# The context side's pool opened in the routing's shadow, in place of an early ring of expert chunks

## The chip, the cores and the metric

The kernel runs on one core of a Trainium2 chip. The metric is the device time in microseconds of one execution, as a median of several runs. All data is fp32. TensorE (PE) multiplies, VectorE (DVE) and ScalarE (ACT) do the elementwise work, GpSimd (POOL) and SyncE (SP) here mostly issue transfers; SP issues those of the weights.

## The reference

Two blocks run one after the other on a sequence of 512 tokens of width 1024, each with a context of 256 tokens. The first block has a mixer (retention, window and neighbourhood attention) and then a feed-forward part with 16 experts, each of which chooses the 64 tokens that it rates highest:

```python
def expert_choice_ffn(h, w_router, w_gate, w_up, w_down):
    ...
    aff = jax.nn.softmax((h @ w_router).astype(jnp.float32), axis=-1)
    gate, idx = lax.top_k(jnp.swapaxes(aff, 1, 2), cap)
    ...
    xe = h[bidx, idx]
    hid = jax.nn.silu(jnp.einsum('becd,edf->becf', xe, w_gate)) * jnp.einsum('becd,edf->becf', xe, w_up)
    ye = jnp.einsum('becf,efd->becd', hid, w_down) * gate[..., None].astype(h.dtype)
    return jnp.zeros_like(h).at[bidx, idx].add(ye)
```

The second block has two layers. In each, the sequence and its own context are normalised and projected, and three branches (latent attention, pooling over 2 to 16 tokens, a gated linear scan) are merged. The first layer also gives a new context to the second. The context side of the first layer needs only the second block's own context input, nothing of the first block.

## The kernel before, in words

The program is written as Python generators that yield the cost of what they have just emitted. `weave(main, fill, ratio)` takes steps from a main generator and, after each, as much from a queue of fill work as the step's cost times the ratio. A scheduler then puts each engine's instructions in an order by its own priorities; each engine works through its queue in that order. Tiles come from pools with a fixed number of buffers for each tag, and a new tile waits until the last user of its buffer is done.

The stages around the change, in order:

- **The mixer of block 1** (`block1_mixer`), in pool `tpA`.
- **The routing** (`ffn_start`, `router`, `topk`). The 8 tiles x are scaled and shifted (L1268 DVE, L1269 ACT), multiplied with the router (L1209, PE), turned, and put through a softmax (L1219 to L1226). Then DVE finds the 64 best tokens of each expert in 8 rounds of MAX, MAX_INDEX and MATCH_REPLACE (L1240 to L1242) and makes indices of them (L1245 to L1257). The tokens are also turned and written to DRAM for the gathers (L1278 to L1282).
- **The experts** (`experts`), in 8 pairs. For each pair a gather fetches the chosen tokens (L1312, POOL), PE turns them (L1322), and 12 groups of matmuls follow (L1307): 4 for each half of gate and up, then 4 for the down projection. A group uses 4 chunks of weights of 512 KB (L1296, SP's queue), 48 chunks in a pair, 384 in all. Expert matmuls have a higher priority than the fill.
- **The context side of the second block's first layer** (`ctx2` with l = 0): input norm (L542, L545, L567 to L570), pooling branch (`poolb`, L1652 to L1672), attention, gated scan, output projection and norm (`finish`, L2002 and L2003). It is the fill of the experts' stage. Its weights come in chunks of 512 KB through a ring of 2 (L412, SP), are split into a high and a low part (L395 ACT, L391 DVE) in rings of 3, and multiplied in three products (L404 to L406), 24 matmuls of 256 columns for a chunk.
- **The join** (`ffn_end`): the experts' sums are turned and added to x (L1417 to L1421), and the first layer of block 2 is normalised (`xstart`).

Before, the expert chunks come from two rings: pool `tpR` holds an early ring of NEARLY = 20 buffers, which serves the first NPRE = 44 chunks, and `bigB` a ring of 8 for the rest. `tpR` stays open until the 44 chunks have been used; in that time experts run without fill. Only then pool `tpB` for the context side opens, and the rest of the experts is woven with it at RATIO_E = 0.8.

Of the kernel before, what the change touches and what calls it, by code (L numbers as in the profile page):

```python
# [7 lines left out]
F32 = mybir.dt.float32  # L8
# [226 lines left out]
def drain(g):  # L235

    while True:
        try:
            next(g)
        except StopIteration as e:  # L240
            return e.value
# [66 lines left out]
def weave(main, fill, ratio):  # L308

    while True:  # L310
        try:
            c = next(main)
        except StopIteration as e:
            return e.value
        fill.step(c * ratio)


class Kern:
# [9 lines left out]
    def pool(s, name, **k):  # L328
        return s.tc.tile_pool(name=name, bufs=1, reuse_waits="tile", **k)
# [956 lines left out]
    def experts(s):  # L1286
# [1 line left out]
        wx = s.d["wexp"]  # L1288

        def chunk(p, i, h):  # L1290
            if s.pre:
                s.pre -= 1
                w = s.early.tile([128, 1024], F32, name=s.uid("we"), tag="early", bufs=NEARLY)
            else:
                w = s.big.tile([128, 1024], F32, name=s.uid("we"), tag="wbig", bufs=s.nbig)
            nc.sync.dma_start(w, wx[p, i][:, h * 1024:h * 1024 + 1024])  # L1296
            return w

        def group(p, c0, stat, ps, kh):

            ws = [[chunk(p, c0 + e, h) for e in (1, 0)][::-1] for h in (1, 0)][::-1]
            with s.tc.high_priority(URGE):
                for h in range(2):
                    for kk in range(2):
                        k = 4 * kh + 2 * h + kk
                        for e in range(2):
                            nc.tensor.matmul(ps[64 * e:64 * e + 64, :], stat[:, k, 64 * e:64 * e + 64],  # L1307
                                             ws[h][e][:, kk * 512:kk * 512 + 512], start=k == 0, stop=k == 7)
# [801 lines left out]
def tags(w=512, **k):  # L2110
    return {a: b if isinstance(b, (tuple, str)) else (b, w) for a, b in k.items()}


PACE = (2, 2.5, 2.5)
NEARLY = 20
URGE = 600
NPRE = 44
LATE = True
XF = 1.0, 1.0
XM = 1.0  # L2120
# [8 lines left out]
GA = 1  # L2129
GX = 4  # L2130
RX = 2.5
TAGS_R = tags(t5=4)
TAGS_0 = tags(1024, u=6)
TAGS_A = tags(t=8, t5="t", y="u", pj=23, hx=16, hc=(16, 256))
TAGS_P = tags(P=(4, 640), PT=(2, 1152))
# [3 lines left out]
TAGS_M = tags(kc=(4, 256), P=(4, 768), PT=4)  # L2139
TAGS_F = tags(fx=8, ft=3)  # L2140
RATIO_G = 2
RATIO_E = 0.8
TAGS_G = tags(gh=8, gl=4)


def body(tc, d, out):
    from contextlib import ExitStack
    with ExitStack() as ctx:
        k = Kern(tc, ctx, d, out)
        pool = lambda n, **kw: ctx.enter_context(tc.tile_pool(name=n, bufs=1, **kw))  # L2150
        k.cp = pool("cp")
        k.wp = pool("wp")
        k.sp = pool("sp")
        k.pp = pool("pp", space=PSUM)
        k.dp = pool("dp", space=bass.MemoryType.DRAM)
        k.setup()
        M, C = [{}, {}], [{}, {}]
        xd, cd = k.dram([8, 128, 512]), k.dram([8, 128, 256])
        yp = pool("yp")
        k.base = (yp, TAGS_0)  # L2160
        with k.pool("tpA") as tp, ExitStack() as c2:
            k.where = (tp, TAGS_A)
            x, r = k.block1_mixer(xd, M, c2)
        k.kp = pool("kp")
        fill = Fill()
        k.nbig, k.pre = 8, NPRE
        big = ExitStack()
        k.big = big.enter_context(k.pool("bigB", side="right"))
        ex = k.experts()
        with k.pool("tpR") as k.early:  # L2170
            k.where = (k.early, TAGS_R)
            drain(k.ffn_start(x, r))
            while k.pre:
                next(ex)
        with k.pool("tpB") as tp:
            k.where = (tp, TAGS_C)
            k.wq = tc.nc.sync
            fill.add(k.ctx2(0, M[0], cd, C[0]))
            weave(ex, fill, RATIO_E)
            big.close()  # L2180
            k.where2 = (big.enter_context(k.pool("fe", side="right")), TAGS_F)
            x, acc = weave(k.ffn_end(xd), fill, RATIO_G)
            fill.flush()
            k.where2 = (None, {})
        k.where = (None, {})
        k.wq = tc.nc.sync
        k.gp = GX
        with k.pool("tpX") as tp:
            k.where = (tp, TAGS_X)
            p = k.xstart(0, M[0], C[0], x, acc, xd, fill, big.close)  # L2190
            f = k.xrest(0, M[0], C[0], *p, xd, None, fill)
            with k.pool("c1") as c1:
                k.where2 = (c1, TAGS_1)
                fill.add(k.ctx2(1, M[1], cd, C[1]))
                x, acc = weave(f, fill, 0.3)
                p = k.xstart(1, M[1], C[1], x, acc, xd, fill)
            k.where2 = (None, {})
            drain(k.xrest(1, M[1], C[1], *p, xd, out, fill))
# [18 lines left out]
```

## Time and profile before

| | us |
|---|---|
| three runs, median | 2788.2 |
| three runs, lowest and highest | 2779.96, 2794.11 |
| the profiled execution | 2794.44 |
| its span, first to last instruction | 2792.6 |

| engine | busy us | share of the span | instructions |
|---|---|---|---|
| PE | 2625.3 | 94% | 16372 |
| DVE | 1569.8 | 56% | 2957 |
| ACT | 1230.6 | 44% | 2159 |
| POOL | 161.0 | 6% | 260 |

PE's share is an average over stages that have different limits, so the stages are to be read one by one. The DMA share is the part of a stretch in which the core's 16 DMA engines were busy, as a mean; near 1 the transfers are the limit. A matmul of the program on fp32 operands of 512 columns shows as two in the trace where the operands are not split.

### The profile page before, as it was taken

How to read it: one execution, taken by the hardware profiler on the slowest of the kernel's cores; microseconds unless marked ns; L12 is line 12 of the kernel's file. 1: busy time of each engine (PE TensorE's matmuls, PEld its weight loads, DVE VectorE, ACT ScalarE, POOL GpSimd, SP SyncE). 2: the span in 40 equal slices, each digit the busy share in tenths (PEclk: the TensorE clock that was granted, in tenths of full speed). 3: DMA queues.
4: the chain of work that ended last, by engine and by line, in shares of the span. 5: the costliest groups of instructions: out<-in, count | busy, mean ns of one | idle time of the engine just before them, and what ended most of it. 6: DMA issues, size and time to landing. Idle time of an engine off the chain costs nothing. (4 is left out here: it accounts for less than half of the span.)

```text
span 2792.6 us, 41759 instructions
## 1 busy us (share of the span) xinstructions
PE 2625.3 (94%) x16372; PEld 1859.9 (67%) x16372; DVE 1569.8 (56%) x2957; ACT 1230.6 (44%) x2159; POOL 161.0 (6%) x260
## 2 busy tenths in 40 slices
PE   6999999999958999999998899999999999999997
PEld 2666677887633566555654577777777777777776
DVE  3564677676441324456232656656866546766974
ACT  3333355444222224365222444545655645555652
POOL 1000001110001000000000000000010000000001
PEclk9899999999979999999999899999999999999998
DMA  8545424634879999988999332213354332114353
GB/s 287 177 164 191 146 85 161 209 120 156 298 283 325 340 380 356 335 297 300 352 366 372 126 106 83 77 51 136 118 186 135 128 123 84 62 39 140 117 177 114
DMA packets 167974, 537.68 MB, mean 193 GB/s; under 512 B 21272, under 2 KB 22376, under 8 KB 167776
## 3 DMA queue, kind: packets, MB, share of 16 engines
q1 hardware_dynamic: 138528, 460.40, 47.2%
q0 software_dynamic: 17152, 52.57, 5.8%
q10 hardware_dynamic: 12096, 22.03, 2.1%
q8 instruction: 129, 2.11, 0.3%
q14 instruction: 69, 0.57, 0.1%
HBM read 484.06 MB, written 48.76 MB: 191 GB/s over the span
## 5 line engine op out<-in xcount | busy, mean ns | idle before, releaser
L391 DVE TENSOR_TENSOR wl<-wr,wh 128x1024 fp32r<-128x1024 f32 x320 | 390.8, 1223 | 386.8 <-ACT wh L395 357.3
L395 ACT CAST wh<-wr 128x1024 fp32r<-128x1024 f32 x320 | 334.4, 1047 | 458.2 <-PE ps L405 348.6
L404 PE MATMUL ps<-hx,wh 128*128 128x512 f32 x1168 | 473.8, 406 | 5.8 <-ACT hx L569 5.1
L405 PE MATMUL ps<-hx,wh 128*128 128x512 f32 x1168 | 468.8, 402 | 0.1
L406 PE MATMUL ps<-hx,wl 128*128 128x512 f32 x1168 | 466.9, 400 | 0.0
L404 PEld LDWEIGHTS ps<-hx,wh 128*128 128x128 f32 x1168 | 221.8, 190 | 66.9 <-issue 13.2
L1307 PE MATMUL ps<-we,xe 128*64 128x512 f32 x1024 | 241.1, 615 | 18.1 <-DMA we<-in_wexp 18.0
L405 PEld LDWEIGHTS ps<-hx,wh 128*128 128x128 f32 x1168 | 221.6, 190 | 52.3 <-issue 8.4
L406 PEld LDWEIGHTS ps<-hx,wl 128*128 128x128 f32 x1168 | 221.7, 190 | 50.2 <-issue 3.3
L673 ACT ACTIVATE P<-ps,st 128x768 f32<-128x768 f32 (+3 forms) x144 | 111.1, 771 | 142.6 <-DVE st L669 107.7
L1307 PEld LDWEIGHTS ps<-we,xe 128*64 128x64 f32 x1024 | 76.0, 141 | 144.8 <-issue 118.4
L404 PE MATMUL ps<-hc,wh 128*128 128x256 f32 x496 | 144.1, 291 | 0.1
L406 PE MATMUL ps<-hc,wl 128*128 128x256 f32 x496 | 139.8, 282 | 0.5 <-DVE wl L391 0.5
L405 PE MATMUL ps<-hc,wh 128*128 128x256 f32 x496 | 140.3, 283 | 0.0
L667 DVE TENSOR_REDUCE st<-ps 128x1 f32<-128x768 f32 (+3 forms) x144 | 114.2, 793 | 38.1 <-PE ps L406 35.3
L1307 PE MATMUL ps<-we,hT 128*64 128x512 f32 x512 | 122.8, 626 | 10.4 <-DMA we<-in_wexp 8.2
L695 PE MATMUL ps<-c_ident,P 128*128 128x128 f32 x688 | 110.0, 278 | 5.3 <-ACT PT L698 3.5
L404 PEld LDWEIGHTS ps<-hc,wh 128*128 128x128 f32 x496 | 94.1, 190 | 19.5 <-issue 14.2
L695 PEld LDWEIGHTS ps<-c_ident,P 128*128 128x128 f32 x688 | 79.9, 140 | 39.8 <-ACT PT L698 13.4
L471 PE MATMUL ps<-wm,sc_cc 128*32 128x512 f32 x384 | 89.4, 647 | 15.9 <-DMA wm<-in_wmod 14.1
L698 ACT COPY PT<-ps 128x512 f32<-128x512 f32 x123 | 70.1, 586 | 72.6 <-PE ps L695 71.9
L405 PEld LDWEIGHTS ps<-hc,wh 128*128 128x128 f32 x496 | 94.0, 190 | 4.0 <-issue 3.5
(517 smaller groups left out, 5036.1 us busy)
## 6 DMA issues: line engine op xcount, KB each, us to landing
we<-in_wexp SPq DMA_DIRECT2D x384, 512.0 KB
wr<-in_win SPq DMA_DIRECT2D x240, 512.0 KB
wm<-in_wmod SPq DMA_DIRECT2D x48, 512.0 KB
wr<-in_wbr SPq DMA_DIRECT2D x48, 512.0 KB
dram<-th ACTq DMA_DIRECT2D x72, 256.0 KB
mth<-dram SPq DMA_DIRECT2D x72, 256.0 KB
wr<-in_wout SPq DMA_DIRECT2D x32, 512.0 KB
dram<-mth POOLq DMA_DIRECT2D x48, 256.0 KB, 3.1
```

The source lines that it names most:

```text
L391: s.nc.vector.tensor_tensor(out, a, b, ALU.subtract)
L395: i = s.nc.scalar.copy(hi, src)
L404: t.matmul(out, a[0], b[0], start=start, stop=False)
L405: t.matmul(out, a[0], b[1], start=False, stop=False)
L406: t.matmul(out, a[1], b[0], start=False, stop=stop)
L471: nc.tensor.matmul(ps[32 * j:32 * j + 32, :], sc[:, k, :], w[:, j % 2 * 512:j % 2 * 512 + 512], start=k == 0, stop=k == 7)
L667: nc.vector.tensor_reduce(st[:, 0:1], sc[:, :n], AX.X, ALU.max)
L673: nc.scalar.activation(p[:, :n], sc[:, :n], AF.Exp, bias=st[:, 1:2], scale=scale, accum_out=st[:, 2:3])
L695: nc.tensor.transpose(tp[:, j:j + 128], blocks[(i + j) // 128], s.const("ident"))
L698: nc.scalar.copy(parts[i // 512][:, :m], tp[:, :m])
L1307: nc.tensor.matmul(ps[64 * e:64 * e + 64, :], stat[:, k, 64 * e:64 * e + 64], ws[h][e][:, kk * 512:kk * 512 + 512], start=k == 0, stop=k == 7)
```

## The change

The early ring and its pool go; all 384 expert chunks come through the ring of 8. The pool `tpB` opens right after the mixer, and the routing (`ffn_start`) is woven with the context side at a new RATIO_R = 0.8. The experts are then woven with it from their first group on, at RATIO_E = 0.55. In the changed program the lines from 1292 on stand 4 lower (L1307 is L1303, L1417 is L1413, L1658 is L1654).

```diff
-            if s.pre:
-                s.pre -= 1
-                w = s.early.tile([128, 1024], F32, name=s.uid("we"), tag="early", bufs=NEARLY)
-            else:
-                w = s.big.tile([128, 1024], F32, name=s.uid("we"), tag="wbig", bufs=s.nbig)
+            w = s.big.tile([128, 1024], F32, name=s.uid("we"), tag="wbig", bufs=s.nbig)
             nc.sync.dma_start(w, wx[p, i][:, h * 1024:h * 1024 + 1024])
...
-NEARLY = 20
...
-NPRE = 44
...
-TAGS_R = tags(t5=4)
...
-RATIO_E = 0.8
+RATIO_E = 0.55
+RATIO_R = 0.8
...
-        k.nbig, k.pre = 8, NPRE
+        k.nbig = 8
         big = ExitStack()
         k.big = big.enter_context(k.pool("bigB", side="right"))
         ex = k.experts()
-        with k.pool("tpR") as k.early:
-            k.where = (k.early, TAGS_R)
-            drain(k.ffn_start(x, r))
-            while k.pre:
-                next(ex)
         with k.pool("tpB") as tp:
             k.where = (tp, TAGS_C)
             k.wq = tc.nc.sync
             fill.add(k.ctx2(0, M[0], cd, C[0]))
+            weave(k.ffn_start(x, r), fill, RATIO_R)
             weave(ex, fill, RATIO_E)
```

DVE's queue at the end of the top-k, before: the last round (wk holds the affinities, vals the best eight) and the first of the index steps.

```order
L1240 MAX vals_6848<-wk_6781 16x8
L1241 MAX_INDEX idx<-vals_6848,wk_6781 16x8
L1242 MATCH_REPLACE wk_6781<-vals_6848,wk_6781 16x512
L1245 CAST idf_6874<-idx 16x64
L1254 TENSOR_SCALAR gate_6876<-ps_6880 64x8
L1255 CAST idx_6877<-ps_6880 64x8
L1256 COPY idxl_6879<-ps_6880 64x1
```

The same place in the changed program; pl, yp, pz and px are tiles of the context's pooling, wl the low part of a context weight.

```order
L1240 MAX vals_6946<-wk_6831 16x8
L1668 SCALAR_TENSOR_TENSOR pl_7090<-ps_7131,vh_6547,gs_7128 128x256
L1241 MAX_INDEX idx<-vals_6946,wk_6831 16x8
L391 TENSOR_TENSOR yp_7135<-pl_7090,yp_7134 128x256
L1242 MATCH_REPLACE wk_6831<-vals_6946,wk_6831 16x512
L1648 MEMSET pz_7177 128x8
L1649 MEMSET pz_7177 128x8
L1245 CAST idf_7191<-idx 16x64
L391 TENSOR_TENSOR wl_7212<-wr_7209,wh_7211 128x1024
L1654 TENSOR_TENSOR px_7181<-pz_7177 128x271
L1254 TENSOR_SCALAR gate_7193<-ps_7197 64x8
L1654 TENSOR_TENSOR px_7183<-px_7181 128x269
```

Between the rounds and the index steps now stand pooling steps and weight splits of the context side, here 7 of 12 rows.

SP's queue, before: the last context weights ahead of the experts' stream (wr is a context weight, we an expert chunk). From the third row on 84 expert chunks follow each other.

```order
L412 DMA wr_7517<-in_win 128x1024
L412 DMA wr_7600<-in_win 128x1024
L1296 DMA we_6912<-in_wexp 128x1024
L1296 DMA we_6914<-in_wexp 128x1024
L1296 DMA we_6916<-in_wexp 128x1024
```

The changed program, from the seventh of its first eight expert chunks to the ninth and tenth.

```order
L1292 DMA we_7290<-in_wexp 128x1024
L1292 DMA we_7292<-in_wexp 128x1024
L412 DMA wr_7209<-in_win 128x1024
L412 DMA wr_7304<-in_win 128x1024
L412 DMA wr_7368<-in_win 128x1024
L412 DMA wr_7445<-in_wbr 128x1024
L412 DMA wr_7464<-in_win 128x1024
L412 DMA wr_7545<-in_win 128x1024
L1292 DMA we_7352<-in_wexp 128x1024
L1292 DMA we_7354<-in_wexp 128x1024
```

Eight expert chunks stand ahead, where 84 stood, and then six context weights, before the stream goes on.

PE's queue at the last expert matmuls (ps<-we), before: behind them comes the join (fo is the sum of the experts, oh, ye and yl the last pair's part).

```order
L1307 MATMUL ps_12837<-we_12871,hT_12258 64x512
L1307 MATMUL ps_12837<-we_12869,hT_12258 64x512
L1417 MATMUL ps_12962<-c_ident,fo_12775 128x128
L1417 MATMUL ps_12962<-c_ident,fo_12777 128x128
L1417 MATMUL ps_12962<-c_ident,fo_12779 128x128
L1417 MATMUL ps_12962<-c_ident,fo_12781 128x128
L516 MATMUL ps_12938<-sq_12959,sqw 2x512
L1419 MATMUL ps_12963<-oh_12773,ye_12783 128x512
L1419 MATMUL ps_12963<-oh_12773,yl_12835 128x512
```

In the changed program: after the last two expert matmuls.

```order
L1303 MATMUL ps_12570<-we_12625,hT_12050 64x512
L1303 MATMUL ps_12570<-we_12623,hT_12050 64x512
L404 MATMUL ps_12668<-mh_12500,wh_12664 128x256
L405 MATMUL ps_12668<-mh_12501,wh_12664 128x256
L406 MATMUL ps_12668<-mh_12500,wl_12665 128x256
L404 MATMUL ps_12668<-mh_12504,wh_12664 128x256
L405 MATMUL ps_12668<-mh_12505,wh_12664 128x256
L406 MATMUL ps_12668<-mh_12504,wl_12665 128x256
```

And further down, where the join begins.

```order
L404 MATMUL ps_12848<-mh_12528,wh_12844 128x256
L405 MATMUL ps_12848<-mh_12529,wh_12844 128x256
L406 MATMUL ps_12848<-mh_12528,wl_12845 128x256
L1415 MATMUL ps_12896<-oh_12415,ye_12425 128x512
L1415 MATMUL ps_12896<-oh_12415,yl_12568 128x512
L1415 MATMUL ps_12916<-oh_12415,ye_12425 128x512
L1415 MATMUL ps_12916<-oh_12415,yl_12568 128x512
L497 MATMUL ps_12878<-ones,sq_12565 128x1 x2
L533 MATMUL ps_12884<-c_ident,rs_12881 128x128 x2
L1413 MATMUL ps_12895<-c_ident,fo_12417 128x128
```

Between these two pieces all rows are of the context's output projection (mh is the merged context, wh and wl a weight's parts): 144 matmuls of 256 columns, which before stood ahead of the last expert matmuls.

## Rows read from the trace of the kernel before

**Rows 1.** Page: the span.
```profile
span 2792.6 us, 41759 instructions
```

**Rows 2.** Stages: us, busy and count of PE, PEld, DVE, ACT, POOL; clock; DMA.
```profile
785.00:833.90 48.90, 19.72 (x96) 11.71 (x94) 25.96 (x69) 15.84 (x24) 2.02 (x2) 0.66 0.97 354
833.90:884.80 50.90, 46.16 (x211) 18.34 (x212) 4.47 (x8) 5.15 (x10) 5.31 (x9) 0.96 0.80 300
884.80:971.80 87.00, 73.43 (x401) 38.62 (x395) 30.24 (x72) 22.40 (x40) 9.69 (x10) 0.94 0.97 334
971.80:1062.10 90.30, 86.92 (x543) 54.50 (x541) 23.97 (x30) 23.46 (x34) 3.94 (x3) 1.00 1.00 378
1062.10:1151.60 89.50, 88.10 (x529) 52.43 (x527) 44.90 (x110) 42.21 (x93) 6.78 (x8) 1.00 0.94 338
1151.60:1252.10 100.50, 94.65 (x697) 55.62 (x697) 47.23 (x120) 51.28 (x109) 4.60 (x4) 0.97 0.90 319
1252.10:1352.80 100.70, 93.42 (x879) 56.10 (x877) 53.96 (x137) 50.47 (x112) 4.16 (x3) 0.97 0.89 310
1352.80:1443.50 90.70, 88.42 (x556) 55.66 (x554) 28.80 (x39) 22.25 (x31) 2.84 (x2) 1.00 0.99 362
1443.50:1536.40 92.90, 82.53 (x470) 46.85 (x470) 28.10 (x50) 24.44 (x44) 9.39 (x14) 0.96 1.01 371
1536.40:1564.60 28.20, 18.81 (x65) 7.33 (x65) 17.79 (x28) 11.03 (x18) 0.00 (x0) 0.83 0.34 121
```

**Rows 3.** Timeline of DVE and ACT in the routing: start, us, engine, line, [idle <-releaser].
```profile
789.61 4.91 DVE L1268 TENSOR_TENSOR x<-x,rb 128x512 f32<-128x512 f32 x8 [1.89 <-ACT rb L1264]
798.97 0.23 DVE L1219 COPY lo<-ps 128x64 f32<-128x64 f32 x1 [4.45 <-PE ps L1214]
...
802.50 0.68 DVE L1240 MAX8 vals<-wk 16x8 f32<-16x512 f32 x1 [1.78 <-ACT wk L1232]
...
822.27 0.17 DVE L1254 TENSOR_SCALAR gate<-ps 64x8 f32<-64x8 f32 x1 [0.70 <-PE ps L1253]
...
822.61 0.17 DVE L1257 CAST idx<-ps 64x16 uint32<-64x16 f32 x1
...
797.83 1.28 ACT L1223 ACT_TABLE_LOAD   x1
```

**Rows 4.** Timeline of PE: the first turn of tokens; one expert group.
```profile
831.99 1.94 PE L1322 MATMUL ps<-c_ident,xg 128*128 128x128 f32 x8 [9.76 <-DMA xg<-dram,idx]
...
1005.42 3.65 PE L1307 MATMUL ps<-we,xe 128*64 128x512 f32 x16 [1.17 <-DMA we<-in_wexp]
```

**Rows 5.** Timeline of PE: first and last of one projection's 24 matmuls.
```profile
1010.53 0.28 PE L404 MATMUL ps<-hc,wh 128*128 128x256 f32 x1
...
1013.24 0.28 PE L406 MATMUL ps<-hc,wl 128*128 128x256 f32 x1
```

**Rows 6.** Groups on DVE, 780 to 1565 us: count | busy, mean ns | idle before.
```profile
L391 DVE TENSOR_TENSOR wl<-wr,wh 128x1024 fp32r<-128x1024 f32 x73 | 89.0, 1224 | 112.9 <-ACT wh L395 100.6 <-PE ps L1307 5.7 <-PE ps L406 5.5
...
L567 DVE SCALAR_TENSOR_TENSOR nf<-c,A,rb 128x256 f32<-128x256 f32 x8 | 3.7, 481 | 1.0 <-ACT rb L557 1.0
L570 DVE SCALAR_TENSOR_TENSOR hc<-nf,mod,hc 128x256 fp32r<-128x256 f32 x8 | 3.7, 479 | 0.0
L2002 DVE SCALAR_TENSOR_TENSOR o<-o,G,rb 128x256 f32<-128x256 f32 x8 | 3.5, 480 | 5.4 <-ACT rb L557 5.4
...
L2003 DVE TENSOR_TENSOR o<-o,xr 128x256 f32<-128x256 f32 x8 | 3.0, 418 | 0.0
...
L1658 DVE TENSOR_TENSOR px<-pz 128x271 f32<-128x271 f32 x4 | 1.8, 440 | 5.2 <-ACT pz L1654 5.2
```

**Rows 7.** Waits of SP's queue in the eight pairs: us, times, longest.
```profile
SPq L1296 <- PE ps L1307: 348.7, 149, 16.6
```

**Rows 8.** Timeline of PE: the join's first turn, the next block's first matmul.
```profile
1540.02 0.66 PE L1417 MATMUL ps<-c_ident,fo 128*128 128x128 f32 x4 [3.64 <-DVE x L1421]
...
1564.58 1.65 PE L404 MATMUL ps<-hx,wh 128*128 128x512 f32 x3 [1.36 <-ACT hx L569]
```

## The prediction

> **What bounds the kernel now.** I read the span first [rows 1], then the table of stages [rows 2], which cuts the trace at the first and last expert matmul and at the end of each of the eight expert pairs. Its first row is the routing: 48.9 us in which PE is busy for 19.7 only, while the DMA engines are busy for 0.97 of the time, because they already fetch expert weights. The next eight rows are the pairs, 702.5 us together (833.9 to 1536.4). There two limits lie side by side. In the third, seventh and eighth pair the DMA engines have a share of 0.99 to 1.01 and move 362 to 378 GB/s: these are DMA bound. In the fourth, fifth and sixth their share falls to 0.89 to 0.94 while PE is busy for 88 of 89.5 us and 93 to 95 of 100: there the context side's work on PE is late. The first two rows (0.80 and 0.97) carry no context matmul at all, or few. The last row is the join after the experts, 28.2 us with PE busy for 18.8. Behind it PE is nearly full in both programs and nothing is moved, so the sum needs three terms: when the first expert matmul starts, how long the eight pairs take, and how long after them the join and what is left of the context take.
>
> A group of 4 chunks (2.1 MB) is 8 matmuls of the program, 16 of the trace, and takes PE 3.65 us [rows 4]; a pair has 12 groups, 43.8 us. A context projection of 24 matmuls of 256 columns runs from 1010.53 to 1013.24, with its last step 0.1165 us each [rows 5], and needs one chunk of 512 KB. DMA time of a chunk at 375 GB/s (the third and eighth pair's rates) is 1.40 us.
>
> **Start of the experts: +23 us.** Before, the chain from the normalised tiles to the first gather is DVE's, hardly with a pause: it starts at 789.61, waits 4.45 us for the logits, begins the top-k at 802.50 and has the index at 822.61 [rows 3]; then the gather keeps PE waiting for 9.76 us [rows 4]. The change puts the context's input norm, three pooling groups and their weight splits on the same DVE queue, in between these steps. DVE works in the order of its queue, so all that stands ahead of a routing step delays it; the later steps of the chain, the gather and the first expert matmul wait behind. Counted from the order, with the durations of [rows 6]:
> - up to the top-k: 8 scalings (0.48 each) and 4 of the 8 low halves (0.48), 5.8 us, and the table load for the exponential, 1.28 us, which ACT did in the wait for the logits [rows 3] and now does after the context's square root. The seven additions of squares fit into the 4.45 us. Sum 7.1.
> - inside the top-k: 4 low halves 1.9, 2 weight splits of 1.22, 11 steps on 256 columns of 0.42 to 0.48 (as L2003 and L567), 4.9, and 10 on a few columns, estimated at 0.1 each: sum 10.2.
> - between top-k and index: 2 weight splits 2.4 and 4 pooling steps and 2 edges, 2.1, less two waits that stood there, the longer 0.70 us: 3.3.
>
> These are 20.6; 2 to 3 us go to new waits on PE and ACT in this chain (pooling alternates between three engines), so **+23**: first expert matmul at 857. Bounds: all added DVE work is 23.7 us, and the chain's pauses (1.89, 4.45, 1.78 and 0.70 [rows 3], 8.8 together) could swallow some of it, so +15; with about a microsecond for each of a dozen handovers, +35. In exchange 144 of the context's matmuls (6 projections, 16.8 us of PE) are done in this shadow. The early ring is gone: 8 chunks of the experts are there at the start, where about 26 were (20 slots and 6 of the other ring).
>
> **The eight pairs: 702.5 to 683, -20 us.** The order of PE gives for each pair the context matmuls of 256 columns and the other small ones between its expert matmuls: before 0, 178, 326, 265, 248, 222, 345, 252; now 192, 216, 203, 193, 96, 180, 240, 228. Together 1548 for 1836: the lower ratio leaves 144 of them for after the experts, and 144 are in front. In chunks the DMA load hardly changes: 18 expert chunks more are still to come, 12 projections fewer, and the context's own inputs come earlier. What changes is that no pair is PE bound by the context's projections now. For each pair I take the larger of two times: PE = 43.8 + 0.1165 per context matmul + 0.125 per other one (from the fifth and sixth pair: 94.65 - 43.8 - 28.9 for 141, and 93.42 - 43.8 - 25.9 for 246); DMA = (chunks x 0.524 MB + 1.5 MB for gathers and scatters) / 375 GB/s. The same rule on the rows of before gives 90.9 for 90.3 (third), 88.4 for 90.7 (seventh), 94.65 for 100.5 and 93.4 for 100.7 (fifth and sixth, the gated scan, where small steps wait for each other): so I add 1.5 us, and 6.5 in the scan's two pairs. Now: chunks 56, 57, 56.5, 56, 52, 55.5, 58 and 49.5 (the last has 8 behind it and 2 MB of results more), DMA 82.3, 83.7, 83.0, 82.3, 76.7, 81.6, 85.0, 78.6; PE 69 to 74 but for the scan, where 222 and 148 other matmuls stand, 82.8 and 83.3. Sum with the additions 83.8 + 85.2 + 84.5 + 83.8 + 89.3 + 89.8 + 86.5 + 80.1 = **683**. The ring of 8 is no new limit: SP already waits for a freed slot 149 times [rows 7] and the third pair ran at 378 GB/s with it. Bounds: all bytes, 245 MB, at 378 GB/s are 648; no gain is 703.
>
> **After the experts: +22 us.** On PE the last 144 context matmuls (6 projections of the output) now stand in one row between the last expert matmul and the join: 16.8 us. Little of the join can run under them, since its matmuls are queued behind; only the 3.64 us in which PE waited for x [rows 8] go. Then the context's last norm comes (a wait of 5.4 us before, by the row of L2002 [rows 6]; ACT has less to do there now, I take 3), and its 16 DVE steps (3.5 + 3.0 us) are interleaved with the join's 16. DVE sets the join's length, so they count: 16.8 - 3.6 + 3 + 6.5 = 22.7, **+22**. Before, this stretch ran from 1536.4 to the first matmul of the next block at 1564.58 [rows 8]. Bounds: 13 (DVE's steps in gaps, and no norm wait) to 25.
>
> **Sum.** 23 - 20 + 22 = +25 us on the profiled execution's 2794.4 us (span 2792.6): 2819. That execution is 6 us above the median of the three runs, 2788.2; on the median the sum is 2813, and this I predict. About 0.5% (14 us) is what a measurement can tell from no change.
>
> **The rivals.**
> 1. *Streaming wins* (faster). The pairs come down to the byte bound, since PE has slack everywhere and small steps of the scan no longer meet full PE queues: 648. With a start at +15 and a join at +18 that gives -22: 2767. For it: the rates of three pairs. Against it: shares of 0.89 in the scan, where the price is waiting, not work. It decides if the pairs take less than about 657 us (then even the other two terms at their low bounds leave a gain). An extreme of it, 0.02 of its chance: DMA is no bound at all, and the pairs take PE's own times, 597 us, with 15 us of waiting: 2788 + 15 - 90 + 18 = 2731. Against that stands the third pair, whose 378 GB/s came with a DMA share of 1.00 [rows 2]. The Trainium skill, Perfetto Trace Analysis, section Roofline, says that a core alone on its memory is bounded by its 16 DMA engines at some 435 GB/s, 120% of its share of 358, which is the price list for this extreme: an estimate of 563 us for the pairs' bytes, less than PE needs. By that rule the engines at 378 still had room; the trace, which calls them fully busy there, doesn't agree.
> 2. *The terms cancel* (no change). DVE's pauses hide more, +15, the pairs take 675, the join +15: +2, 2790. For it: the pieces of PE work are the same in both, so only idle time can differ, and the idle routing is a third of what is idle in this stretch.
> 3. *The shadow is too short* (slower still). SP's queue now has six context weights between the first 8 expert chunks and the rest; they wait for split buffers, and with them the experts' stream. If the start comes at +35 and the pairs gain 10 only, +47: 2835.
> 4. *The change does nothing in the shadow*: the new pool's tiles wait for the tiles of the mixer that they replace. Then PE gets nothing before 833 and the lost prefetch, 18 chunks x 1.40 = 25 us, is the price: 2813, no other number than mine.
>
> **How the numbers follow.** Forecast with 4: 0.48; streaming wins 0.15; cancel 0.27; too short 0.10. Slower 0.58, same 0.27, faster 0.15. The range leaves out most of the first rival and the far end of the third: 2779 to 2838; the forecast's own is 2803 to 2826.
>
> **What would show it.** Right: the first expert matmul about 20 us or more after the routing's present end, DVE without a pause through it; DMA share in the routing well under 0.97; the scan's pairs near 89 us; 144 narrow matmuls in a row behind the last expert matmul, and some 50 us to the next block. Wrong: an index at most 10 us later; pairs of under 81 us; join steps of DVE that finish within 30 us.

## The result, and the profile after

The changed kernel takes 2816.8 us (median of 4 runs, 2815.7 to 2818.0), the kernel before 2791.2 in the runs beside it: a ratio of 1.0097, 95% interval 1.0073 to 1.0122. It is slower by about 26 us, where 25 were forecast. The profiled execution took 2815.7 us; from the page:

```profile
span 2813.8 us, 41706 instructions
```

The same table of stages as [rows 2] (stretch, its length, busy time and count of PE, PEld, DVE, ACT and POOL, granted clock, DMA share, GB/s), cut at the same events of the changed kernel: the routing, the eight pairs, and the stretch from the last expert matmul to the next block's first matmul.

```profile
783.00:845.80 62.80, 42.94 (x252) 34.02 (x250) 48.26 (x132) 31.52 (x57) 9.76 (x16) 0.79 0.60 198
845.80:920.30 74.50, 71.67 (x412) 39.17 (x411) 15.68 (x25) 12.99 (x20) 0.95 (x1) 0.99 0.97 351
920.30:1002.60 82.30, 74.74 (x429) 41.61 (x430) 18.93 (x24) 22.11 (x34) 3.87 (x3) 1.00 1.00 376
1002.60:1091.70 89.10, 81.69 (x455) 44.11 (x455) 36.40 (x96) 30.61 (x73) 6.76 (x8) 0.98 0.94 336
1091.70:1183.20 91.50, 82.76 (x442) 43.28 (x442) 27.53 (x56) 34.86 (x66) 4.64 (x4) 0.94 0.93 328
1183.20:1281.80 98.60, 81.02 (x716) 43.43 (x718) 49.51 (x139) 44.14 (x103) 3.88 (x3) 0.90 0.84 299
1281.80:1364.40 82.60, 78.24 (x641) 44.39 (x639) 30.37 (x73) 30.82 (x63) 3.89 (x3) 1.00 0.99 357
1364.40:1445.30 80.90, 74.75 (x440) 42.98 (x440) 20.29 (x28) 16.28 (x23) 2.84 (x2) 1.00 1.01 386
1445.30:1534.10 88.80, 77.49 (x429) 42.15 (x430) 23.95 (x35) 21.17 (x34) 7.73 (x11) 0.96 0.98 363
1534.10:1588.00 53.90, 41.21 (x226) 28.97 (x226) 31.33 (x56) 21.87 (x37) 1.61 (x3) 0.90 0.43 150
```

Read against [rows 2], the span's 21.2 us are four differences: the first expert matmul starts 11.9 us later (845.8 for 833.9), the eight pairs take 14.2 less (688.3 for 702.5), the stretch behind them 25.7 more (53.9 for 28.2), and all that follows 2.2 less. The medians lie 4 us further apart than these two executions.

**The routing.** DVE's busy time from its first routing step to the top-k, through the top-k, and from there to the index (columns: DVE, clock, DMA share, GB/s), before:

```profile
789.61:802.50 12.89, 6.20 (x14) 0.76 1.01 391
802.50:820.62 18.12, 17.33 (x40) 0.69 0.93 337
820.62:822.61 1.99, 0.80 (x8) 0.50 1.07 393
```

and in the changed kernel:

```profile
787.58:807.04 19.46, 13.78 (x35) 0.68 0.65 246
807.04:833.88 26.84, 24.45 (x67) 0.83 0.49 152
833.88:838.78 4.90, 4.79 (x19) 1.00 0.42 129
```

DVE's chain is 51.2 us long instead of 33.0, with 121 instructions in it instead of 62. Its idle time hardly changes (8.2 us for 8.7): what is added is work. The timeline of DVE shows how the context's steps lie in it (start, us, engine, line, operands, idle before and releaser):

```profile
805.06 0.47 DVE L567 SCALAR_TENSOR_TENSOR nf<-c,A,rb 128x256 f32<-128x256 f32 x1
805.46 0.47 DVE L570 SCALAR_TENSOR_TENSOR hc<-nf,mod,hc 128x256 fp32r<-128x256 f32 x1
805.85 0.47 DVE L567 SCALAR_TENSOR_TENSOR nf<-c,A,rb 128x256 f32<-128x256 f32 x1
...
807.04 0.68 DVE L1240 MAX8 vals<-wk 16x8 f32<-16x512 f32 x1
...
830.87 0.42 DVE L578 SCALAR_TENSOR_TENSOR gs<-gs,ps 128x256 f32<-128x256 f32 x1 [1.59 <-ACT gs L577]
...
833.88 0.17 DVE L1245 CAST idf<-idx 16x64 f32<-16x64 uint32 x1
...
838.78 0.17 DVE L1257 CAST idx<-ps 64x16 uint32<-64x16 f32 x1
```

The first three rows last 0.47 us each and start 0.40 us apart: a step's time in the trace overlaps the next one's start. The row of 830.87 is one of few waits: a context step waits for ACT, and the top-k's next round stands behind it.

PE behind the index, with the wait for the gathered tokens that was 9.76 us in [rows 4]:

```profile
843.92 1.94 PE L1318 MATMUL ps<-c_ident,xg 128*128 128x128 f32 x8 [4.68 <-DMA xg<-dram,idx]
845.79 2.57 PE L1303 MATMUL ps<-we,xe 128*64 128x512 f32 x8
```

**Behind the experts.** The stretch in three pieces (columns as in the table of stages), and PE's timeline in it:

```profile
1534.10:1544.00 9.90, 6.32 (x50) 5.91 (x50) 3.32 (x5) 4.27 (x7) 1.08 (x2) 0.97 0.85 319
1544.00:1558.10 14.10, 13.96 (x95) 13.96 (x96) 6.37 (x9) 6.54 (x11) 0.54 (x1) 0.78 0.53 174
1558.10:1588.00 29.90, 20.93 (x83) 9.10 (x82) 21.65 (x44) 11.06 (x20) 0.00 (x0) 0.94 0.24 82
```

```profile
1542.88 0.39 PE L404 MATMUL ps<-mh,wh 128*128 128x256 f32 x1 [2.97 <-ACT wh L395]
...
1544.14 0.58 PE L406 MATMUL ps<-mh,wl 128*128 128x256 f32 x1 [0.76 <-DVE wl L391]
1544.52 0.42 PE L404 MATMUL ps<-mh,wh 128*128 128x256 f32 x1
1544.74 0.42 PE L405 MATMUL ps<-mh,wh 128*128 128x256 f32 x1
...
1557.46 0.28 PE L405 MATMUL ps<-mh,wh 128*128 128x256 f32 x1
1557.58 0.28 PE L406 MATMUL ps<-mh,wl 128*128 128x256 f32 x1
...
1588.01 1.65 PE L404 MATMUL ps<-hx,wh 128*128 128x512 f32 x3 [1.36 <-ACT hx L569]
```

The 144 narrow matmuls fill 1534.1 to 1558.1: 24.0 us, and the join behind them takes 29.9, where it took 28.2 alone. Twice PE waits for a weight (2.97 and 0.76 us). After the waits the matmuls start 0.21 us apart, at 1557 they start 0.117 apart: the granted clock of the second piece is 0.78, a mixture of the two levels (1.2 and 2.4 GHz).

### The profile page after: what moved, and what is told of

Its sections match the earlier page's. It is cut to its first block, busy times and chain, and to the rows that moved or that the text cites. A ratio compares the mean times of both kernels' runs of the same rounds, so it can differ in the third digit from the quotient of the medians.

```text
span 2813.8 us, 41706 instructions
## 1 busy us (share of the span) xinstructions
PE 2636.4 (94%) x16372; PEld 1865.2 (66%) x16372; DVE 1566.8 (56%) x2957; ACT 1228.9 (44%) x2155; POOL 159.5 (6%) x260
## 5 line engine op out<-in xcount | busy, mean ns | idle before, releaser
L1303 PE MATMUL ps<-we,xe 128*64 128x512 f32 x1024 | 243.2, 616 | 31.9 <-DMA we<-in_wexp 30.7
L1303 PEld LDWEIGHTS ps<-we,xe 128*64 128x64 f32 x1024 | 72.5, 141 | 161.3 <-issue 123.4
L1303 PE MATMUL ps<-we,hT 128*64 128x512 f32 x512 | 122.4, 623 | 6.1 <-DMA we<-in_wexp 4.3
L404 PEld LDWEIGHTS ps<-hc,wh 128*128 128x128 f32 x496 | 96.3, 195 | 32.9 <-issue 25.6
L406 PEld LDWEIGHTS ps<-hc,wl 128*128 128x128 f32 x496 | 96.3, 194 | 5.4 <-DVE wl L391 4.2
```

The source lines that it names most:

```text
L404: t.matmul(out, a[0], b[0], start=start, stop=False)
L406: t.matmul(out, a[1], b[0], start=False, stop=stop)
```

## The experiments

The theory: three terms add up. The routing becomes longer on DVE's queue and the prefetch is lost; the pairs have a floor in their bytes, so that less fill in them saves only part of its work; and what is left over behind the experts is paid in full. Ratios are against the kernel before, in runs beside each; differences to the changed kernel are between medians. Rows are of one execution of each kernel, whose routing can begin some us earlier or later than another's.

### The leftover put back among the experts

```diff
-RATIO_E = 0.55
+RATIO_E = 0.6
```

> The changed kernel with one number other: the fill's share in the experts is 0.60 instead of 0.55, so that none of the 144 narrow context matmuls is left over behind the experts; they lie within the eight pairs, most of them in the second half. Theory (the three terms add; the leftover is paid in full, a pair pays for fill only where its PE work is above its bytes or its waits): from the end of the experts to the next block's first matmul 54 us falls to 28 to 32; the eight pairs grow from 688 by 0 to 10 us; the start stays within 2 us of 846; 2817 - 24 + 6 = about 2799. Rival (PE's work is conserved, so the 144 cost the same wherever they stand): pairs grow by 17 to 24, about 2814.

Measured: 2801.0 us, ratio 1.0040 (1.0025 to 1.0056), 15.8 below the changed kernel. The pairs, and the stretch behind them:

```profile
844.30:1545.80 701.50, 640.96 (x4111) 359.09 (x4110) 234.20 (x501) 223.35 (x436) 36.49 (x38) 0.97 0.95 346
1545.80:1574.00 28.20, 17.41 (x67) 7.16 (x65) 18.69 (x31) 10.19 (x17) 0.00 (x0) 0.85 0.48 167
```

The 53.9 us are 28.2 again, exactly the length before. The pairs grow by 13.2, more than the theory's 0 to 10 and less than the rival's 17 to 24. So one narrow matmul costs 0.092 us among the experts (13.2 / 144) and 0.178 behind them (25.7 / 144). The time agrees with the theory, though the pairs hide less than it said. The higher ratio also moves other fill from later pairs to earlier ones, so the two prices are averages.

### The spread taken away

```diff
-RATIO_E = 0.55
+RATIO_E = 0.8
```

> The changed kernel with 0.80 instead of 0.55 as the fill's share in the experts, as in the kernel before: the fill is used up after six of the eight pairs, and nothing is left over behind them. It takes the spread away and keeps the pool's early opening. Theory (a pair costs the larger of its bytes and its PE work, and pairs without fill cannot go under their bytes, 78 to 80 us): the first six pairs grow by 60 to 80 us together against share 0.60, the last two shrink by 15 to 20; pairs 725 to 740 instead of 701, 28 us behind them, 2820 to 2838. Rival (only the sum of the work counts, not its spread): 2801, as with 0.60.

Measured: 2842.1 us, ratio 1.0192 (1.0169 to 1.0215). The fourth pair, the last two, and all eight:

```profile
1118.50:1233.20 114.70, 100.03 (x969) 60.36 (x969) 62.19 (x172) 61.08 (x142) 4.16 (x3) 0.90 0.78 266
1422.30:1504.50 82.20, 54.47 (x212) 17.25 (x211) 9.53 (x21) 5.76 (x9) 4.75 (x5) 0.90 0.95 331
1504.50:1585.50 81.00, 55.23 (x212) 18.09 (x212) 4.76 (x7) 5.83 (x8) 5.08 (x6) 0.89 0.91 329
844.70:1585.50 740.80, 652.76 (x4111) 364.47 (x4110) 236.63 (x505) 226.05 (x440) 37.03 (x38) 0.95 0.93 329
```

The same 4111 matmul records as with 0.60, and 39.3 us more in the pairs. Against 0.60 the first six pairs take 52 more (577.6 for 525.5, where 60 to 80 were expected) and the last two 13 less (163.2 for 176.0, where 15 to 20 were). The rival falls: the place of the fill counts. A pair without fill has PE busy for 55 us and still takes 81 to 82, 10 more than my prediction's rule for 48 chunks (26.7 MB at 375 GB/s, 71). The ring of 8 streams at 330 GB/s there, and PE waits for chunks for 48.2 us in the two pairs. The time is 4 us above the expected range.

### Nothing in the shadow

```diff
-RATIO_E = 0.55
-RATIO_R = 0.8
+RATIO_E = 0.634
+RATIO_R = 0.0
```

> The changed kernel without any fill in the routing's shadow (share 0 there), and 0.634 in the experts so that about the same is left over behind them (168 narrow matmuls). Theory (the shadow's fill makes the routing longer on VectorE's queue and earns little later): the first expert matmul is 10 to 14 us earlier (832 to 836), the pairs 5 to 12 us longer than 688, the leftover's 24 more matmuls 3 us: about 2816, the same as the changed kernel. Rival (the shadow's fill is worth its PE time, 144 matmuls of 0.117 us and the splits with it): about 2833. Second rival (the shadow only costs): 2805.

Measured: 2820.2 us, ratio 1.0108 (1.0090 to 1.0125), 3.4 above the changed kernel, with intervals that overlap. Routing, pairs, and the stretch behind:

```profile
785.00:831.30 46.30, 18.38 (x80) 10.87 (x80) 27.96 (x72) 16.39 (x29) 4.21 (x7) 0.62 0.55 201
831.30:1531.60 700.30, 637.40 (x4082) 353.49 (x4081) 243.74 (x529) 225.57 (x440) 37.33 (x38) 0.98 0.95 344
1531.60:1591.80 60.20, 45.69 (x253) 32.72 (x251) 32.66 (x57) 23.92 (x40) 2.15 (x4) 0.83 0.44 149
```

The start comes 14.5 us earlier, the pairs are 12.0 longer, and the 24 further leftover matmuls cost 6.3 (I had put 3). That is the theory: the shadow gives about as much in the pairs as it takes in the routing. The 3.4 us are no more than the larger leftover costs, so the fill in the shadow is worth nothing that can be measured.

### The routing's steps first

```diff
-            nc.vector.max(vals[0:16, q], wk[0:16])
+            with s.tc.high_priority(URGE):
+                nc.vector.max(vals[0:16, q], wk[0:16])
...
```

All top-k and index steps on DVE (L1240 to L1257), and the four small matmuls between them (L1252, L1253), get the expert matmuls' priority, so that they stand ahead of the fill.

> The changed kernel with the routing's top-k and index steps put ahead of the fill's splits in VectorE's order; the same fill in each stretch. Theory (the splits between the top-k steps lengthen the routing, and the routing is the path): the top-k part falls from 26.8 us towards the 18.1 of the kernel before, the index from 838.8 to 829 to 833, the first expert matmul from 845.8 to 837 to 840; the pairs keep 688 within 3: about 2810. Rival (the experts are bound by bytes that could not arrive earlier, so an earlier start only adds waiting in the first pairs): the pairs grow by the 6 to 8 us gained, 2817.

Measured: 2816.4 us, ratio 1.0090 (1.0075 to 1.0106): no gain that is shown. The index comes 5.6 us earlier, near what the theory wanted, 1.0 of it because the routing itself begins 1.0 earlier:

```profile
833.17 0.17 DVE L1261 CAST idx<-ps 64x16 uint32<-64x16 f32 x1
```

But the first expert matmul starts at 844.35, only 1.4 earlier. PE's queue:

```profile
842.30 0.67 PE L1672 MATMUL ps<-pl,pw 128*128 128x256 f32 x2
842.81 0.60 PE L1323 MATMUL ps<-c_ident,xg 128*128 128x128 f32 x4
844.35 1.94 PE L1308 MATMUL ps<-we,xe 128*64 128x512 f32 x8 [0.94 <-DVE xe L1324]
```

PE now goes from the context's matmuls straight into turning the gathered tokens, with no wait for them. They had landed at 838.8, 4.0 us before: the fill in PE's queue is what came last. Both theory and rival miss the place: the earlier index was eaten between the index and the first expert matmul, not in the first pairs. These rows are of the fastest of the six executions (2809.9 us); its pairs are 4.5 us shorter than the changed kernel's (683.8 for 688.3), a gain that the medians do not show.

### The prefetch alone

```diff
-NEARLY = 20
+NEARLY = 8
```

in the kernel before.

> The kernel before with one thing of the change alone: the early ring has 8 buffers instead of as many as fitted, so 12 of the chunks that were in memory before the first expert matmul are not; the fill is spread as before. Theory (the experts' stretch is bound by bytes, so each chunk fetched ahead is worth its transfer): the first expert matmul stays within 3 us of 834; the pairs grow from 702 by 12 x 1.40 = 17 us; about 2808. Rival (the pairs are bound by PE and by waits on it, the prefetch is immaterial): 2791 within 4.

Measured: 2808.9 us, ratio 1.0061 (1.0043 to 1.0079), the time that the theory had. The first pair, all pairs, and PE's wait for the gather:

```profile
829.00:898.80 69.80, 51.51 (x211) 16.92 (x212) 4.47 (x8) 5.36 (x10) 5.87 (x10) 0.91 0.83 295
829.00:1549.60 720.60, 659.17 (x4267) 377.67 (x4266) 261.73 (x566) 242.01 (x472) 45.23 (x53) 0.97 0.95 339
```

```profile
827.14 1.94 PE L1322 MATMUL ps<-c_ident,xg 128*128 128x128 f32 x8 [5.77 <-DMA xg<-dram,idx]
```

The pairs grow by 18.1, all of it in the first (69.8 for 50.9). PE waits for chunks there for 16.6 us instead of 4.1, and the expert matmuls take 49.1 instead of 43.9, at a granted clock of 0.91 instead of 0.96. By the first expert matmul 16 chunks had been issued, where before 26 had: 10 fewer, and not 12, so 1.40 us for each would be 14. At the same time the wait for the gather falls from 9.76 [rows 4] to 5.77, and the first expert matmul comes 4.9 us earlier (829.0), which the theory, with 834 within 3, did not have.

### Both: the prefetch kept, the pool opened earlier

```diff
-NPRE = 44
+NPRE = 20
...
-RATIO_E = 0.8
+RATIO_E = 0.72
```

in the kernel before; the second kernel has 28 and 0.74.

> The kernel before, with its early ring of 20 buffers, but each buffer used once (20 chunks instead of 44 pass it), so that the context's pool opens inside the first pair rather than behind it, and 0.72 instead of 0.80 as the fill's share, so that the fill spreads over more of the experts and none is left over. Theory (prefetch is worth 1.40 us a chunk, spreading is worth something only where a pair is bound by PE, the routing stays free of fill): the first expert matmul at 829 to 834, the eight pairs 688 to 703, 28 us to the next block: 2775 to 2790. Rival (the fill's spread is worth nothing): 2790 within 4. Second rival (more chunks ahead delay the gather's rows further): start 838, 2795.

> As b_p20 with 28 chunks through the early ring and 0.74 as the fill's share: the context's pool opens about two thirds into the first pair. Theory: between the kernel before and b_p20, 2778 to 2790. Rival (opening inside the first pair costs a wait of the ring): above 2795.

Measured: 2798.0, ratio 1.0033 (1.0019 to 1.0047), and 2785.7, ratio 0.9987 (0.9971 to 1.0003). The first is a miss. Its experts start at 830.6, as the theory had it and not at the second rival's 838, but its first pair takes 65.1 us instead of 50.9, and the wait for the gather is longer too:

```profile
828.76 1.94 PE L1322 MATMUL ps<-c_ident,xg 128*128 128x128 f32 x8 [12.02 <-DMA xg<-dram,idx]
```

PE's waits for chunks in the first pair, in the kernel with 20, in that with 28, and in the kernel before (line, releaser: us, times, longest):

```profile
PE ps L1307 <- DMA we<-in_wexp: 10.5, 3, 4.1
PE ps L1307 <- DMA we<-in_wexp: 3.9, 1, 3.9
PE ps L1307 <- DMA we<-in_wexp: 4.1, 1, 4.1
```

By the first expert matmul 28, 26 and 26 chunks had been issued, so the longer waits do not come from less being fetched ahead. With 20 the early buffers are not used again, and SP issues nothing between 821.9 and 851.0; before, and with 28, the next chunk goes out at 836.4 and 835.3. So the early ring is worth its buffers by their second use in the first pair, and not only by what it fetched ahead. These waits are 6.4 of the 14.2 us. The rest is fill in that pair (24 context matmuls and those of the input norm, 4.0 us) and expert matmuls at a lower granted clock (47.5 us for 43.9, at 0.90 for 0.96).

With 28 the first pair holds no context projection, just as before, and takes 56.9. That is not for want of chunks: PE waits 2.1 us for the context's input norm, whose matmuls take 1.2, and the expert matmuls take 46.0 us at a clock of 0.91.

In the kernel with 20 the seven other pairs gain 7.7 us (643.9 for 651.6), and the stretch behind loses 4.3 (32.5 for 28.2). With 28 the time is the lowest of all here, but its interval holds 1: no gain that is shown. Its profiled execution, 2794.1 us, is one of its slower ones.

### The join's steps first

```diff
         for k in range(9):
+            up = s.tc.high_priority(URGE)
+            up.__enter__()
             if k < 8:
...
                 s.sqrow(ps, x[k - 1], w[:, k - 1, :], k - 1, "ft")
+            up.__exit__(None, None, None)
```

The turning, the additions to x (L1413, L1415, L1417), the squares and, in the same way, the norm's steps behind them get the expert matmuls' priority.

> The changed kernel with the steps of the experts' end (combine, residual, norm) put ahead of the leftover's splits in VectorE's order; the 144 narrow matmuls stay behind the experts. Theory (in the 54 us the matmuls take 24, and the splits between the end's steps 6 to 8): the 54 us become 45 to 49, 2809 to 2813. Rival (the matmuls and their weights' splits are the path and the end's steps have slack): 54 stays, 2817. The floor, if the matmuls hid wholly under the end's steps: 28, 2791.

Measured: 2811.1 us, ratio 1.0080 (1.0058 to 1.0101), in the range of the theory, though the interval overlaps with the changed kernel's; and the stretch shrinks by 3.0 only (50.9, where 45 to 49 were expected). In two pieces, up to the last narrow matmul and from there:

```profile
1535.80:1559.00 23.20, 19.82 (x149) 19.22 (x148) 10.39 (x13) 10.85 (x17) 1.61 (x3) 0.93 0.71 245
1559.00:1586.70 27.70, 19.78 (x82) 9.65 (x80) 21.02 (x44) 11.18 (x20) 0.00 (x0) 0.88 0.25 85
```

The matmuls take 23.2 (24.0 in the changed kernel) and the join 27.7 (29.9), one after the other as before. So the interleaved DVE steps cost 2 us, not the 6 to 8 of the expectation, and the matmuls' own row is the rest. The other 3 us of the 5.7 lie outside this stretch and are not explained.

## Why the prediction was right, point by point

**The whole.** Slower by 26 us with 25 forecast, and the three terms have their signs and their order: start +11.9 (forecast +23), pairs -14.2 (-20), behind the experts +25.7 (+22). The sum is closer than its parts: the start was too high by 11, the two others too low by 6 and 4. That these errors cancel to 2 us is luck. Along the experiments' medians the change is a smaller ring, +19 (2789.8 to 2808.9); the pool opened early, with the fill in the shadow and over all pairs, -8 (to 2801.0); and 144 matmuls left over, +16 (to 2816.8). The first two steps are not pure: with the small ring 16 chunks are issued ahead, in the changed kernel 8.

**Start, the term most mis-sized.** The chain on DVE came out as counted in kind: 18.2 us longer where 20.6 were summed: 6.6 up to the top-k (7.1), 8.7 in it (10.2), 2.9 behind (3.3). Each piece is a little short of the sum, since durations of the trace overlap the next start (0.47 long, 0.40 apart); for the 59 added instructions that is a few us. The 2 to 3 us for new waits were no extra: they took the place of old pauses (8.2 us idle for 8.7). What the sum lacked is the gather. I carried its 9.76 us over unchanged, although I wrote that the early ring's transfers would be gone: from the index to the first expert matmul there are now 7.0 us instead of 11.3, and the first gather lands 4.8 us after its issue instead of 8.4. The kernel with the small ring and no other change shows the same, 7.3, and the one with more fetched ahead shows 13.5. The Trainium skill, DMA: Bandwidth & Descriptors, section Queues, rings and completion order, says that each DMA engine takes turns between its queues packet by packet, by which a gather shares the engines with the stream; PE's waits of 4.68 and 5.77 us with a thinner stream and of 9.76 and 12.02 with a full one agree in direction, and no run shows single packets. The last 2 us of the start lie ahead of the change's steps: the routing itself begins 2.0 us earlier, and in the eight other kernels' traces it begins between 784.2 and 790.4, so this difference may be chance.

**The pairs.** 688.3 for 683. The rule of the larger of two times is borne out where the bytes were the larger (the second and seventh run at 376 and 386 GB/s with a DMA share of 1.00 and 1.01), but three things in it were off, and partly cancelled. First, the ring's 8 chunks were subtracted at the wrong end: they are there before the first pair, which moved 26.1 MB in 74.5 us (83.8 forecast), and the last moved 32.2 in 88.8 (80.1). The trace has 41 expert chunks landing in the first pair and 45 in the last. Second, PE was busy for 82 and 83 us in the third and fourth pair, where the rule gives 75 and 73. Counted from each matmul's start to the next one's, or to its own end before a pause, the 60 and 57 other matmuls took 0.16 us each (0.125 in the rule), which is 2 us in each pair. The context's took 0.135 and 0.131 (0.1165 in the rule), 3.6 and 2.7 us more, and the experts' 44.9 and 47.5 us (43.8 in the rule), at granted clocks of 0.98 and 0.94. So the price of all three kinds was low, not that of the other matmuls alone. Third, the waits: 7.4, 8.7 and 17.6 us without PE in the third to fifth pair, where I allowed 1.5, 1.5 and 6.5. These three pairs took 21.6 more than forecast, the second, sixth and seventh 15.7 less. The price of the scan was uncertain from the start: the 94.65 and 93.4 that the prediction gives as the rule's for the two pairs before are PE's busy times in [rows 2]; the rule with 0.125 gives 90.3 and 100.5 there.

**Behind the experts.** The mechanism is shown: with the leftover gone, the stretch has its old length. The two parts were both off. The matmuls were priced at 16.8 and took 24.0, with 3.7 of waits for weights and the rest at the lower clock; SP issued these weights late, behind eight loads of x and through the ring of 2:

```profile
1527.49 8.17 SPq L1401 DMA_DIRECT2D x<-dram  x8
1535.76 8.69 SPq L412 DMA_DIRECT2D wr<-in_wout  x3
```

The DVE steps and the norm wait were priced at 5.9 on balance (3 + 6.5 - 3.6) and cost 1.7. The prediction let DVE set the join's length, but DVE was idle for 10.4 of the 28.2 us before (17.8 busy [rows 2]) and is busy for 21.7 of 29.9 now: most of the added steps found gaps.

**The rivals.** That streaming wins falls: the pairs took 688, not under 657. (With the two other terms at their low bounds, 15 and 13, a gain would begin under 674; 657 goes with terms of 23 and 22.) That the terms cancel falls with the leftover: without it 11 us remain (2801). The shadow was not too short: the start came early, not late. The fourth rival, that the change does nothing in the shadow, had the forecast's number for another reason; the 144 matmuls are in the shadow, so it is wrong as told, but the kernel without fill there takes 2820, so its price was not far off. Of what should have shown each step, DVE without a pause holds for the top-k and the index (29.2 of 31.7 us busy) and not ahead of them (13.8 of 19.5); the DMA share of the routing is 0.60; the scan's pairs were 98.6 and 82.6 rather than 89 each; and the first expert matmul came 12 us after its old place instead of 20 or more, so that sign did not hold. The 144 matmuls in a row, the 54 us to the next block and an index 16 us later are as told. Of the signs of being wrong, one came in part: two of the eight pairs, the first and the seventh, took under 81 us (74.5 and 80.9).

## What to carry to other kernels

Work that a change leaves over behind a stage should be priced at its full length plus the start of its own supply; among work that waits for transfers the same matmuls cost half as much here. A prefetch ring pays by what it fetches ahead and again by each later use of its buffers, and what it fetches can delay other transfers: when it goes, count the shorter waits too. An idle stretch of one engine is not free when the fill also passes the queue of the engine that is busy there; moving the urgent steps ahead on that one queue only handed the wait to the next here.

## What was not expected of the hardware

How long the first gather takes from issue to landing goes with the stream beside it: 4.8, 4.4 and 4.7 us (the changed kernel, the one with the small ring, the one without fill in the shadow) where the DMA share between the index and the first expert matmul was 0.78, 0.49 and 0.35; 8.4, 8.4 and 9.0 (the kernel before, and those with 28 and 20 uses of the early ring) where it was 0.99 to 1.02. Among the first three it does not follow the share. From the index to the first expert matmul this makes 7.0, 7.3 and 8.4 us, and 11.3, 11.3 and 13.5. Pairs that nothing else occupies do not reach the rates of the busy ones: 329 and 331 GB/s with a ring of 8 and PE busy for 55 of 81 us, against 376 and 386 in pairs that carry fill, whose context weights come through a second ring.
